# The row of 1/rms spread through DRAM instead of identity products, with a re-ordered start, in a two-layer encoder trunk

## The chip, the core and the metric

The kernel runs on one core of one Trainium2 chip. The metric is device time in microseconds for one launch; a figure for several runs is their median.

## What is computed

A trunk of two layers over 512 tokens of width 1024, all in float32. Each layer normalizes x, projects it to four branches and their gates, mixes them back and adds, then does the same with a convolutional feed-forward block:

```python
def _rmsnorm(x, g):
    y = xf * lax.rsqrt(jnp.mean(jnp.square(xf), axis=-1, keepdims=True) + EPS)
    return (y * g).astype(x.dtype)

for l in range(DEPTH):                      # DEPTH = 2, SEQ = 512, D_MODEL = 1024
    h = _rmsnorm(x, g_mix[l])
    proj = h @ w_in[l]                      # gates, conformer GLU, q/k/v of three attentions
    ...
    x = x + mixed @ w_out[l]
    x = x + _conv_ffn(_rmsnorm(x, g_ffn[l]), w_up[l], ffn_conv_w[l], ffn_conv_b[l], w_down[l])
```

## The kernel before

The activations stand transposed: eight tiles of 128 channels by 512 tokens. Each float32 operand is split into a rounded part and a remainder (xh and xl, w_hi and w_lo), and each product is made of three matmuls, hi by hi, hi by lo and lo by hi (L224 to L226, token-major L408 to L410).

**Weights** come in units of 128x1024 (`weights`, L189): a DMA into w_raw (two buffers), ScalarE rounds to w_hi (L204), VectorE subtracts to w_lo (L205), three buffers each. One unit feeds one block of 24 matmuls of 512 columns. `unit` (L209) keeps the next unit requested. The DMAs stand on SyncE's queue (SP), except the very first unit's, which comes in two halves on ScalarE's queue. Tiles of a pool with bufs=n go round in n buffers, and a writer waits for the readers of the buffer's last use. PSUM holds eight tiles of 128x512: four of mm, four of aux.

**Norms.** The factor 1/rms of a token is not applied to x; the products are made of x times the gain, and the factor is multiplied in behind them. `norm_tile` (L264) makes xh and xl of each tile and gathers the squares in sqacc. `finish_norm` (L281) sums sqacc over partitions with four matmuls by a column of ones (L293), so that token b*128+p stands on partition p, column b, and takes the inverse root on VectorE (`rsqrt`, L242): rstd, 128x4. Where tokens lie on partitions, rstd is used as it is. Where tokens lie along the row, in `glu`, `gates` and `ffn`, the factor is needed as RB, 128x512, the same row on each partition: before, VectorE scaled the identity by each column of rstd (L300), TensorE multiplied these four 128x128 tiles by the identity (L306), and ScalarE copied the result from PSUM to RB (L308). RB and sqacc share one buffer. `finish_norm` is called four times: at the start, between the mixing and the feed-forward in each layer, and at the start of layer 1. It is a generator, and `tick` (L731) advances all such side tasks: once in the middle of a block, once or more behind it. With delay 1 at a feed-forward the sums of squares come behind the first block.

**Feed-forward** (`ffn`, L776). Blocks come in pairs, gate and up. After each pair VectorE reads both PSUM tiles times RB into U (L796, shown below), ScalarE and VectorE do the three-tap convolution (L799 to L801), then swish and the product. Each block and the sums of squares take the next of the four mm tiles.

```python
                ps = pss[s]
                u = U[(2 * i + s) % 4]
                v.tensor_tensor(u[:, 1:513], ps, self.RB, ALU.mult)
```

**The start** (`run`, L817). ScalarE loads its table with a dummy exponential, POOL zeroes a tile z, and TensorE multiplies z by itself WARM times. x tile 0, sixteen columns of the parameters (the gains), x tile 1 and the others come on SP's queue. The order of instructions on each engine is set by a scheduler that follows the program's order and priorities; `issue_after` and the high priority of the weights shift it.

Of the kernel before, what the change touches and what calls it, by code (L numbers as in the profile page):

```python
# [14 lines left out]
F32 = mybir.dt.float32  # L15
F32R = mybir.dt.float32r
I32 = mybir.dt.int32
AF = mybir.ActivationFunctionType
ALU = mybir.AluOpType
# [3 lines left out]
P = 128  # L23
L = 2
D = 1024
S = 512
KT = D // P
NB = S // P
# [18 lines left out]
NCST = 1544  # L47


WARM = 9  # L50


PHASE = 24
# [127 lines left out]
class Trunk:  # L181
# [7 lines left out]
    def weights(self, upto, ahead=3000, parts=1, queue=None):  # L189

        nc = self.nc
        while self.w_emitted < min(upto, len(self.w_list)):
            l, off, n = self.w_list[self.w_emitted]
            with self.tc.high_priority(offset=ahead):
                raw = self.wpool.tile([P, 1024], F32, name="w_raw", tag="w_raw", bufs=2)
                hi = self.wpool.tile([P, 1024], F32R, name="w_hi", tag="w_hi", bufs=3)
                lo = self.wpool.tile([P, 1024], F32R, name="w_lo", tag="w_lo", bufs=3)
                src = self.W[l, off:off + n * P].rearrange("(p c) -> p c", p=P)
                for i in range(parts):
                    s = slice(i * n // parts, (i + 1) * n // parts)  # L200
                    (queue or nc.sync).dma_start(raw[:, s], src[:, s])
                for i in range(parts):
                    s = slice(i * n // parts, (i + 1) * n // parts)
                    nc.scalar.activation(hi[:, s], raw[:, s], AF.Copy)  # L204
                    nc.vector.tensor_tensor(lo[:, s], raw[:, s], hi[:, s].bitcast(F32), ALU.subtract)  # L205
            self.w_ready.append((hi, lo))
            self.w_emitted += 1
# [56 lines left out]
    def norm_tile(self, d, xn, pool):  # L264

        nc = self.nc
        g = self.par(self.norm_g, d)
        xh = self.xpool.tile([P, S], F32R, name=f"xh{d}", tag=f"xh{d}", bufs=1)
        xl = self.xpool.tile([P, S], F32R, name=f"xl{d}", tag=f"xl{d}", bufs=1)
        nc.scalar.activation(xh, xn, AF.Copy, scale=g)  # L270
        nc.vector.scalar_tensor_tensor(xl, xn, g, xh.bitcast(F32), ALU.mult, ALU.subtract)
        self.Xh.append(xh)
        self.Xl.append(xl)
        if d == 0:
            nc.scalar.activation(self.sqacc, xn, AF.Square)
        else:
            sq = pool.tile([P, S], F32, name="sq", tag="sq", bufs=2)
            nc.scalar.activation(sq, xn, AF.Square)
            nc.vector.tensor_tensor(self.sqacc, self.sqacc, sq, ALU.add)

    def finish_norm(self, delay):  # L281

        nc = self.nc
        sqacc = self.sqacc
        self.rstd = self.norm.tile([P, NB], F32, name="rstd", tag="rstd", bufs=2)
        rstd = self.rstd

        def work():
            for _ in range(delay):
                yield  # L290
            ps = self.mm()
            for b in range(NB):
                nc.tensor.matmul(ps[:, b:b + 1], lhsT=sqacc[:, b * P:(b + 1) * P],  # L293
                                 rhs=self.cst[:, C_ONE:C_ONE + 1], start=True, stop=True)
            v = self.norm.tile([P, NB], F32, name="ms", tag="ms", bufs=2)
            nc.vector.tensor_scalar(v, ps[:, 0:NB], 1.0 / D, EPS, ALU.mult, ALU.add)
            self.rsqrt(self.norm, v, [P, NB], rstd)
            dg = self.scratch()
            for b in range(NB):
                nc.vector.tensor_scalar(dg[:, b * P:(b + 1) * P], self.ident, 0.0, rstd[:, b:b + 1], ALU.mult, ALU.add)  # L300
            yield
            yield
            ps = self.aux()
            for b in range(NB):
                t = slice(b * P, (b + 1) * P)
                nc.tensor.matmul(ps[:, t], lhsT=dg[:, t], rhs=self.ident, start=True, stop=True)  # L306
            self.RB = self.norm.tile([P, S + PHASE], F32, name="RB", tag="RB", bufs=1)[:, :S]
            nc.scalar.activation(self.RB, ps, AF.Copy)  # L308
            yield

        self.side.append(work())
# [505 lines left out]
    def run(self):  # L817
        nc, tc = self.nc, self.tc
        with ExitStack() as st:
            pool = lambda name, **k: st.enter_context(tc.tile_pool(name=name, bufs=1, **k))  # L820
            self.const = pool("const")
            self.xpool = pool("xparts")
            self.wpool = pool("weights")
            self.norm = pool("norm")
            self.psum = pool("psum", space=PSUM)
            self.dram = pool("dram", space=bass.MemoryType.DRAM)
            self.w_list = []
            for l in range(L):
                off = 0
                for _, _, n in UNITS:  # L830
                    self.w_list.append((l, off, n))
                    off += n * P
            self.w_emitted = self.w_used = 0
            self.w_ready = []
            self.side, self.waiting, self.head = [], [], None

            self.cst = self.const.tile([P, NCST], F32, name="cst", tag="cst", bufs=1)
            self.ident = self.cst[:, C_ID:C_ID + P]
            self.prm = self.const.tile([P, NPAR], F32, name="prm", tag="prm", bufs=1)
            warm = self.const.tile([P, 1], F32, name="warm", tag="warm", bufs=1)  # L840
            nc.vector.memset(warm, 0.0)
            nc.scalar.activation(warm, warm, AF.Exp)
            with tc.tile_pool(name="first", bufs=1, reuse_waits="tile") as first:

                z = first.tile([P, S], F32R, name="zero", tag="zero", bufs=1)
                nc.gpsimd.memset(z.bitcast(F32), 0.0)
                ps = self.aux()
                for i in range(WARM):
                    nc.tensor.matmul(ps, lhsT=z[:, :P], rhs=z, start=True, stop=True)
                self.start_norm('g_mix')  # L850
                for d in range(KT):
                    xn = first.tile([P, S], F32, name="xn", tag="xn", bufs=8)
                    nc.sync.dma_start(xn, self.xT[d])
                    if d == 0:
                        nc.sync.dma_start(self.prm[:, 0:16], self.PAR[0][:, 0:16])
                        self.weights(1, 0, 2, nc.scalar)
                    self.norm_tile(d, xn, first)
                    if d in (1, 3):
                        self.weights(2 + d // 2, 0)
                    if d == 2:  # L860
                        nc.sync.dma_start(self.prm[:, 16:], self.PAR[0][:, 16:])
                nc.sync.dma_start(self.cst, self.CST)
                self.finish_norm(7)
            self.xres = [self.xT[d] for d in range(KT)]
            for l in range(L):
                self.layer(l)
# [5 lines left out]
    def layer(self, l):  # L872
# [2 lines left out]
        self.Y, self.mixed, self.MH, self.glu_u = [None] * 4, [], [], []  # L875
        with tc.tile_pool(name="gate", bufs=1, reuse_waits="tile") as self.gp:
            with tc.tile_pool(name="attn", bufs=1, reuse_waits="tile") as self.ap:
                self.scratch = lambda: self.gp.tile([P, S], F32, name="dg", tag="t1", bufs=2)
                late = lambda n: iter([None] * n)
                Q = self.project_qk(None, self.aux)  # L880
                self.derive_params()
                V = self.new_V()
                self.queue(chain(late(3 if l else 5), self.qk_norm(*Q, 4, 4, 0), self.attention(l, 'na', V, 1)))
                Vd = self.new_V()
                self.project_v(V, Vd)
                Q = self.project_qk(0)
                self.queue(chain(self.qk_norm(*Q, 4, 4, 2), self.attention(l, 'dil', Vd, 2)))
                self.glu()
                self.side.append(self.conv())
                V = self.new_V()  # L890
                Q = self.project_swa(V)
                self.queue(chain(self.qk_norm(*Q, 4, 2, 4), self.attention(l, 'swa', V, 3)))
                for n in ORDER[:3]:
                    self.gates(n)
                while self.side:
                    self.tick()
            with tc.tile_pool(name="outp", bufs=1, reuse_waits="tile") as self.op:
# [3 lines left out]
                for d in range(0, KT, 2):  # L901
# [3 lines left out]
                    for k0, k1 in zip(cuts, cuts[1:]):  # L905
                        for e in range(2):
                            if k0 == 0:
                                ws.append(self.unit())
                            hi, lo = ws[e]
# [6 lines left out]
                self.xres = self.xnew  # L916
                self.finish_norm(1)
        with tc.tile_pool(name="ffn", bufs=1, reuse_waits="tile") as self.fp:
            self.scratch = lambda: self.fp.tile([P, S], F32, name="dg", tag="cy0", bufs=2)
            F = self.ffn()  # L920
            if not last:
                self.load_prm(l + 1)
# [57 lines left out]
```

## Time and profile before

| | us |
|---|---|
| median of three runs | 1604.56 |
| lowest, highest | 1604.18, 1605.97 |
| the profiled execution, its own time | 1605.87 |
| span in its profile | 1604.1 |
| TensorE busy, matmuls | 1594.7 (99%) |
| VectorE, ScalarE, POOL busy | 1110.1, 778.6, 99.9 |

Times in the profile are microseconds from the first instruction; a matmul's time runs until its pipeline is empty, so starts, not durations, tell the pace of TensorE. DVE is VectorE, ACT ScalarE, SP SyncE, POOL GpSimd, PE TensorE; a name with q is the engine's sequencer, which also issues DMAs. L12 is line 12 of the kernel before; behind the change lines are numbered anew.

### The profile page before, as it was taken

The numbers are of one execution on the slowest core, as the hardware profiler recorded it, in microseconds if no ns is written. First come the engines' busy times: TensorE is split into PE (matmuls) and PEld (weight loads), VectorE is DVE, ScalarE is ACT, GpSimd is POOL, SyncE is SP. The second block draws the span as 40 slices with busy tenths as digits, with TensorE's granted clock in tenths as the row PEclk, the third lists the DMA queues.
The fourth block names the chain that finished last, engine by engine and source line by source line (L and its number), as shares of the span: only waits on it lengthen the run. The fifth ranks groups of instructions, "written<-read, shape, count | busy, mean of one in ns | idle before, by whom it ended". The sixth has DMA issues, their size and how long they took to land.

```text
span 1604.1 us, 19934 instructions
## 1 busy us (share of the span) xinstructions
PE 1594.7 (99%) x7425; PEld 1328.0 (83%) x7425; DVE 1110.1 (69%) x1860; ACT 778.6 (49%) x1303; POOL 99.9 (6%) x169
## 2 busy tenths in 40 slices
PE   9999999999999999999999999999999999999999
PEld 7888888888888888888888888888888888888887
DVE  6689888765677777843356889887556777777221
ACT  5677766433444444432237777662434444444211
POOL 0012001222000000000000110012210000000000
PEclk9999999999999999999999999999999999999999
DMA  6523232333533233233336322223326333333342
GB/s 206 182 92 90 71 88 78 93 97 97 181 112 104 93 94 104 89 128 129 126 111 182 105 67 87 83 66 105 105 93 187 106 102 92 102 95 91 122 135 74
DMA packets 57041, 174.95 MB, mean 109 GB/s; under 512 B 6768, under 2 KB 7024, under 8 KB 56944
## 3 DMA queue, kind: packets, MB, share of 16 engines
q1 hardware_dynamic: 56656, 173.16, 34.7%
q8 instruction: 58, 0.95, 0.2%
q10 hardware_dynamic: 288, 0.52, 0.1%
q14 instruction: 39, 0.32, 0.1%
HBM read 157.93 MB, written 10.49 MB: 105 GB/s over the span
## 4 chain that ended last, share of the span: by engine, by line
PE 92%; DVE 4%; ACT 2%; issue 1%; DMA 0%; SPq 0%; ACTq 0%; DVEq 0%
PE mm L224 25%; PE mm L226 25%; PE mm L225 25%; PE mm L408 2%; PE mm L410 2%; PE mm L409 2%; PE aux L629 1%; DVE w_lo L205 1%; PE aux L408 1%; PE aux L409 1%; PE aux L410 1%; PE aux L653 1%; PE aux L592 1%; PE aux L652 1%; PE aux L593 1%
## 5 line engine op out<-in xcount | busy, mean ns | idle before, releaser
L224 PE MATMUL mm<-xh,w_hi 128*128 128x512 f32 x1280 | 500.1, 391 | 0.0
L226 PE MATMUL mm<-xh,w_lo 128*128 128x512 f32 x1280 | 499.0, 390 | 0.0
L225 PE MATMUL mm<-xl,w_hi 128*128 128x512 f32 x1280 | 498.6, 390 | 0.0
L204 ACT ACTIVATE w_hi<-w_raw 128x1024 fp32r<-128x1024 f32 (+2 forms) x273 | 284.5, 1042 | 421.4 <-PE mm L225 344.3
L205 DVE TENSOR_TENSOR w_lo<-w_raw,w_hi 128x1024 fp32r<-128x1024 f32 (+2 forms) x273 | 330.1, 1210 | 160.3 <-ACT w_hi L204 156.4
L226 PEld LDWEIGHTS mm<-xh,w_lo 128*128 128x128 f32 x1280 | 240.3, 188 | 50.7
L224 PEld LDWEIGHTS mm<-xh,w_hi 128*128 128x128 f32 x1280 | 240.3, 188 | 49.2 <-ACT V L530 0.3
L225 PEld LDWEIGHTS mm<-xl,w_hi 128*128 128x128 f32 x1280 | 240.4, 188 | 48.6
L224 PE MATMUL mm<-fh,w_hi 128*128 128x512 f32 x352 | 136.9, 389 | 0.0
L225 PE MATMUL mm<-fl,w_hi 128*128 128x512 f32 x352 | 136.9, 389 | 0.0
L226 PE MATMUL mm<-fh,w_lo 128*128 128x512 f32 x352 | 136.9, 389 | 0.0
L346 DVE SCALAR_TENSOR_TENSOR cv<-cv,prm 128x512 f32<-128x512 f32 x120 | 93.6, 780 | 0.6
L723 POOL TENSOR_TENSOR mx<-mx,t 128x512 f32<-128x512 f32 x44 | 66.9, 1529 | 422.7 <-DVE t L722 413.8
L811 ACT ACTIVATE fh<-cy 128x512 fp32r<-128x512 f32 x44 | 27.8, 632 | 117.6 <-DVE cy L808 117.6
L765 DVE TENSOR_TENSOR xn<-mm,xr 128x512 f32<-128x512 f32 x32 | 22.1, 691 | 84.3 <-PE mm L226 81.2
L226 PEld LDWEIGHTS mm<-fh,w_lo 128*128 128x128 f32 x352 | 66.1, 188 | 13.8
L224 PEld LDWEIGHTS mm<-fh,w_hi 128*128 128x128 f32 x352 | 66.1, 188 | 13.7
L225 PEld LDWEIGHTS mm<-fl,w_hi 128*128 128x128 f32 x352 | 66.1, 188 | 13.7
L408 PE MATMUL mm<-w_hi,xh 128*128 128x512 f32 x192 | 76.4, 398 | 0.3 <-DVE V L531 0.2
L693 DVE TENSOR_TENSOR t<-mm,RB 128x512 f32<-128x512 f32 x64 | 44.0, 687 | 46.2 <-PE mm L226 45.8
L410 PE MATMUL mm<-w_hi,xl 128*128 128x512 f32 x192 | 75.1, 391 | 0.0
L409 PE MATMUL mm<-w_lo,xh 128*128 128x512 f32 x192 | 74.9, 390 | 0.0
(145 smaller groups left out, 2296.8 us busy)
## 6 DMA issues: line engine op xcount, KB each, us to landing
w_raw<-W SPq DMA_DIRECT2D x239, 512.0 KB, 3.6
w_raw<-W SPq DMA_DIRECT2D x32, 448.0 KB, 3.4
res<-xn SPq DMA_DIRECT2D x24, 256.0 KB, 2.0
xr<-res SPq DMA_DIRECT2D x24, 256.0 KB, 2.9
tab<-TB SPq DMA_DIRECT2D x8, 448.0 KB, 3.8
KH<-KH SPq DMA_DIRECT2D x20, 128.0 KB, 3.9
KL<-KL SPq DMA_DIRECT2D x20, 128.0 KB, 3.9
xn<-xT SPq DMA_DIRECT2D x8, 256.0 KB, 5.4
```

The lines of the kernel that those rows point to most:

```text
L204: nc.scalar.activation(hi[:, s], raw[:, s], AF.Copy)
L205: nc.vector.tensor_tensor(lo[:, s], raw[:, s], hi[:, s].bitcast(F32), ALU.subtract)
L224: mm(ps, lhsT=wh, rhs=xh, start=start, stop=False)
L225: mm(ps, lhsT=wh, rhs=xl, start=False, stop=False)
L226: self.last_mm = mm(ps, lhsT=wl, rhs=xh, start=False, stop=stop)
L346: self.after_mm(v.scalar_tensor_tensor(acc, u[:, t:t + S], w(t), acc, ALU.mult, ALU.add))
L408: mm(pss[b], lhsT=self.Xh[k][:, t], rhs=hi[:, s], start=k == 0, stop=False)
L409: mm(pss[b], lhsT=self.Xh[k][:, t], rhs=lo[:, s], start=False, stop=False)
L410: self.last_mm = mm(pss[b], lhsT=self.Xl[k][:, t], rhs=hi[:, s], start=False, stop=k == KT - 1)
L693: v.tensor_tensor(t1, ps, self.RB, ALU.mult)
L723: (v if n == ORDER[3] and d >= 6 else nc.gpsimd).tensor_tensor(m, m, t, ALU.add)
L811: nc.scalar.activation(fh, f, AF.Copy, scale=0.5)
```

## The change

The identity products, their scratch tile and ScalarE's copy are gone. POOL issues two DMAs instead: rstd into a row of 512 values in DRAM, and that row back to all 128 partitions of RB. At the start the sixteen parameter columns are issued on ScalarE's queue, ahead of the first weight's halves, instead of on SP's; the dummy exponential is placed behind those halves in the program; z is zeroed by VectorE; there are ten warm products instead of nine; and the square of x tile 0 is issued behind the first w_hi.

```diff
-WARM = 9
+WARM = 10
...
-                    nc.scalar.activation(hi[:, s], raw[:, s], AF.Copy)
+                    w = nc.scalar.activation(hi[:, s], raw[:, s], AF.Copy)
+                    self.first_hi = self.first_hi or w
...
         if d == 0:
-            nc.scalar.activation(self.sqacc, xn, AF.Square)
+            with self.tc.issue_after(self.first_hi.ins):
+                nc.scalar.activation(self.sqacc, xn, AF.Square)
...
-            dg = self.scratch()
-            for b in range(NB):
-                nc.vector.tensor_scalar(dg[:, b * P:(b + 1) * P], self.ident, 0.0, rstd[:, b:b + 1], ALU.mult, ALU.add)
-            yield
-            yield
-            ps = self.aux()
-            for b in range(NB):
-                t = slice(b * P, (b + 1) * P)
-                nc.tensor.matmul(ps[:, t], lhsT=dg[:, t], rhs=self.ident, start=True, stop=True)
+            row = self.dram.tile([S], F32, name="row", tag="row", bufs=2)
+            nc.gpsimd.dma_start(row.rearrange("(b p) -> p b", p=P), rstd)
             self.RB = self.norm.tile([P, S + PHASE], F32, name="RB", tag="RB", bufs=1)[:, :S]
-            nc.scalar.activation(self.RB, ps, AF.Copy)
+            nc.gpsimd.dma_start(self.RB, row.unsqueeze(0).broadcast_to([P, S]))
...
+            nc.scalar.dma_start(self.prm[:, 0:16], self.PAR[0][:, 0:16])
             warm = self.const.tile([P, 1], F32, name="warm", tag="warm", bufs=1)
             nc.vector.memset(warm, 0.0)
-            nc.scalar.activation(warm, warm, AF.Exp)
...
-                nc.gpsimd.memset(z.bitcast(F32), 0.0)
+                nc.vector.memset(z.bitcast(F32), 0.0)
...
                     if d == 0:
-                        nc.sync.dma_start(self.prm[:, 0:16], self.PAR[0][:, 0:16])
                         self.weights(1, 0, 2, nc.scalar)
+                        nc.scalar.activation(warm, warm, AF.Exp)
```

On ScalarE at the start, before (w_raw halves are the first weight unit, xh_105 and xh_112 are x tiles 0 and 1):

```order
L201 DMA w_raw<-W 128x512
L842 ACT_TABLE_LOAD
L842 ACTIVATE warm<-warm 128x1
L201 DMA w_raw<-W 128x512
L270 ACTIVATE xh_105<-xn,prm 128x512
L275 ACTIVATE sqacc<-xn 128x512
L204 ACTIVATE w_hi<-w_raw 128x512
```

and after the change:

```order
L836 DMA prm<-PAR 128x16
L201 DMA w_raw<-W 128x512
L852 ACT_TABLE_LOAD
L852 ACTIVATE warm<-warm 128x1
L201 DMA w_raw<-W 128x512
L271 ACTIVATE xh_106<-xn,prm 128x512
L204 ACTIVATE w_hi<-w_raw 128x512
L277 ACTIVATE sqacc<-xn 128x512
```

The parameters come in front of the weight's first half, and the square moves behind w_hi.

On VectorE at the feed-forward of layer 0, before (rstd is the last step of the inverse root, U_4529 and U_4532 are the first pair's tiles):

```order
L252 SCALAR_TENSOR_TENSOR rstd<-rs_q,rstd 128x4
L300 TENSOR_SCALAR dg<-cst,rstd 128x128 x4
L205 TENSOR_TENSOR w_lo<-w_raw,w_hi 128x1024
L796 TENSOR_TENSOR U_4529<-mm,RB 128x512
L796 TENSOR_TENSOR U_4532<-mm,RB 128x512
```

and after the change:

```order
L253 SCALAR_TENSOR_TENSOR rstd<-rs_q,rstd 128x4
L206 TENSOR_TENSOR w_lo<-w_raw,w_hi 128x1024
L791 TENSOR_TENSOR U_4522<-mm,RB 128x512
L791 TENSOR_TENSOR U_4525<-mm,RB 128x512
L795 SCALAR_TENSOR_TENSOR cy_4621<-U_4522,prm,cy_4621 128x512
L795 SCALAR_TENSOR_TENSOR cy_4629<-U_4525,prm,cy_4629 128x512
L796 SCALAR_TENSOR_TENSOR cy_4621<-U_4522,prm,cy_4621 128x512
L206 TENSOR_TENSOR w_lo<-w_raw,w_hi 128x1024
```

Only the scalings are gone in front of the first read of RB; one w_lo stands ahead of it, the next one five instructions behind.

On POOL at the same place, after the change (the memsets are the borders of the U tiles):

```order
L778 MEMSET U_4531 128x1
L301 DMA row<-rstd 128x4x1
L303 DMA RB<-row 128x512
L313 MEMSET cv 128x15
```

Before, the memset of U was followed directly by that of cv, which belongs to layer 1.

## Rows read from the trace of the kernel before

**Rows 1.** The page, part 1: busy us (share of the span) xinstructions, TensorE's matmuls.

```profile
PE 1594.7 (99%) x7425; PEld 1328.0 (83%) x7425; DVE 1110.1 (69%) x1860; ACT 778.6 (49%) x1303; POOL 99.9 (6%) x169
```

**Rows 2.** Waits of PE: engine line waited for: us in total, times, longest us.

```profile
PE aux L408 <- ACT w_hi L204: 1.2, 1, 1.2
```

**Rows 3.** Timeline of PE, first feed-forward: start us, us, engine line op out<-in.

```profile
455.26 0.39 PE L226 MATMUL mm<-xh,w_lo 128*128 128x512 f32 x1
455.49 1.05 PE L306 MATMUL aux<-cst,dg 128*128 128x128 f32 x8
456.30 0.48 PE L224 MATMUL mm<-xh,w_hi 128*128 128x512 f32 x1
...
461.84 0.39 PE L224 MATMUL mm<-xh,w_hi 128*128 128x512 f32 x1
```

**Rows 4.** Timeline of PE, start of layer 1.

```profile
823.87 0.39 PE L408 MATMUL aux<-w_hi,xh 128*128 128x512 f32 x1
...
825.05 0.48 PE L409 MATMUL aux<-w_lo,xh 128*128 128x512 f32 x1
```

**Rows 5.** Chain of waits, 0 to 14 us: start us, us, what.

```profile
1.18 3.60 DMA prm<-PAR
...
5.58 0.52 ACT sqacc L275
6.10 0.53 ACT w_hi L204
```

**Rows 6.** Timeline of ScalarE, first DMA issue.

```profile
0.73 0.41 ACTq L201 DMA_DIRECT2D w_raw<-W  x1
```

**Rows 7.** Timeline of PE, first 12 us; in brackets idle before, releaser.

```profile
1.30 4.21 PE L849 MATMUL aux<-zero 128*128 128x512 f32 x9 [1.30 <-POOL zero L846]
6.67 2.08 PE L408 MATMUL aux<-w_hi,xh 128*128 128x512 f32 x4 [1.16 <-ACT w_hi L204]
...
9.83 0.63 PE L410 MATMUL aux<-w_hi,xl 128*128 128x512 f32 x1
10.26 0.53 PE L409 MATMUL aux<-w_lo,xh 128*128 128x512 f32 x1
10.62 0.39 PE L410 MATMUL aux<-w_hi,xl 128*128 128x512 f32 x1
...
11.54 0.40 PE L409 MATMUL aux<-w_lo,xh 128*128 128x512 f32 x1
```

**Rows 8.** Stretches: length, busy of five engines, granted clock, DMA share, GB/s.

```profile
6.67:10.30 3.63, 3.62 (x9) 2.86 (x10) 3.63 (x8) 3.63 (x7) 0.00 (x0) 1.00 1.03 359
450.00:460.00 10.00, 10.00 (x49) 8.39 (x49) 6.93 (x21) 3.31 (x5) 0.00 (x0) 1.00 0.31 93
```

**Rows 9.** Timeline of VectorE, first feed-forward.

```profile
453.29 0.16 DVE L252 SCALAR_TENSOR_TENSOR rstd<-rs_q,rstd 128x4 f32<-128x4 f32 x1
...
456.60 1.23 DVE L205 TENSOR_TENSOR w_lo<-w_raw,w_hi 128x1024 fp32r<-128x1024 f32 x1 [2.24 <-ACT w_hi L204]
457.75 1.28 DVE L796 TENSOR_TENSOR U<-mm,RB 128x512 f32<-128x512 f32 x2
```

**Rows 10.** DMA issues: out<-in, queue, count, KB each, median us to landing.

```profile
res<-xn SPq DMA_DIRECT2D x24, 256.0 KB, 2.0
xr<-res SPq DMA_DIRECT2D x24, 256.0 KB, 2.9
...
V<-turn SPq DMA_DIRECT2D x2, 1024.0 KB, 5.8
...
w_raw<-W ACTq DMA_DIRECT2D x2, 256.0 KB, 3.9
...
prm<-PAR SPq DMA_DIRECT2D x1, 8.0 KB, 3.6
```

**Rows 11.** Timeline of VectorE, first 12 us.

```profile
7.94 0.68 DVE L205 TENSOR_TENSOR w_lo<-w_raw,w_hi 128x512 fp32r<-128x512 f32 x1
```

**Rows 12.** Timeline of POOL, before the first feed-forward.

```profile
405.30 0.10 POOL L783 MEMSET U<- 128x1 f32 x1
```

More of the change, by code (lines that the diff above doesn't have):

```diff
@@ L833, in run @@
             self.w_emitted = self.w_used = 0
+            self.first_hi = None
             self.w_ready = []
@@ L877, in layer @@
             with tc.tile_pool(name="attn", bufs=1, reuse_waits="tile") as self.ap:
-                self.scratch = lambda: self.gp.tile([P, S], F32, name="dg", tag="t1", bufs=2)
                 late = lambda n: iter([None] * n)
@@ L918, in layer @@
         with tc.tile_pool(name="ffn", bufs=1, reuse_waits="tile") as self.fp:
-            self.scratch = lambda: self.fp.tile([P, S], F32, name="dg", tag="cy0", bufs=2)
             F = self.ffn()
```

## The prediction

> **What bounds the kernel now.** I read the busy shares first, then what TensorE waited for, then the timeline at the places that the change touches. TensorE (PE) is busy for 1594.7 of 1604.1 us [rows 1], so an edit is worth something only if it shortens PE's own stream or makes PE wait. The list of PE's waits is short, and its longest single entries are at the start: 1.2 us for the first rounded weight [rows 2], and 1.30 before that for the zeroed tile [rows 7]; both lie in code that the change rewrites. The third kind of place is the identity products (L306). In the timeline at the first feed-forward block they are issued at 455.49, and the next product starts at 456.30 and takes 0.48 where its neighbours take 0.39 [rows 3]: they stand in PE's stream, not beside it. So there are three things to price: those products, the start, and the one place where the new route can make PE wait.
>
> **The identity products go.** Without them the product at 456.30 would start at 455.49: 0.81 us, and 0.09 for the long one behind it, 0.90 in all [rows 3]. In layer 1's start they split a triple: 823.87 to 825.05 is 1.18 where neighbours are 0.23 apart, so 0.95 and again 0.09, 1.04 [rows 3, 4]. The four places give 3 x 0.90 + 1.04 = **3.7 us**. The four VectorE scalings (L300) and ScalarE's copy (L308) go too; PE waits for neither, so I give them nothing.
>
> **The start.** The chain at the start reads: the small parameter DMA from 1.18 for 3.60 us, xh, the square, w_hi, then PE [rows 5]. The change puts that DMA first on ScalarE's queue, at 0.73 where the weight's first half is issued now [rows 6], so it would land 0.45 us earlier at the same 3.60; and the square moves behind w_hi, which takes its 0.52 out. The weight's half moves back one slot, from 0.73 to about 1.18, and with its 3.9 us [rows 10] it lands at about 5.1. That is just when xh would be done (6.67 - 0.45 - 0.52 = 5.70 for PE; less w_hi's 0.53 and 0.04 of hand-over is 5.13), so it holds w_hi by 0.05 to 0.1. PE's first real product comes at about 5.8 instead of 6.67: **0.9 us**, with 0.4 as the lower end if the extra DMA ahead of it merely delays the half (the DMA share just behind is already 1.03 [rows 8]), and 1.0 as the upper.
>
> The memset of z moves from POOL to VectorE behind a 128x1 memset, so PE's warm products may start some 0.1 later than 1.30. They are ten at 0.43 instead of nine, so they end near 5.7, where the real work begins. This matters only to the clock. The products from 6.67 on are 0.43 apart until 10.26, then 0.36 and from there 0.23, four steps from 10.62 to 11.54 [rows 7]: the ratio of 1.2 to 2.4 GHz, although the granted clock's column prints 1.00 [rows 8]. Eight steps of 0.43 and one of 0.36 cost 8 x 0.2 + 0.13 = 1.7 us over the fast pace. Before them PE worked from 1.30 to 5.51 and then stood idle for 1.16 us. With the gap closed the rise may come before the real work (1.7 gained) or as late after its start as now (nothing). No row shows an unbroken start, so I take the middle, **0.9 us**. The Trainium skill (TensorE: Matmul & The Clock Gate, section "Part 1: The HAM clock gate") says that activity releases the throttle and idleness brings it back; by that rule the closed gap would give back most of the 1.7, and the sum below would be 0.8 lower. The trace agrees as far as it goes: the rise came only in unbroken work behind the gap.
>
> Can PE be fed that much earlier? It would run up to 2.6 us ahead. The tightest input that I find is the second half's w_lo, which ends at 8.62 and is read by the product at 11.54 [rows 7, 11]: 2.9 us of slack. It holds, barely. SP's queue is also re-ordered (one slot less in front, one x tile ahead of two weights); those shifts are 0.45 us per slot and stay inside the same slack.
>
> **The detour through DRAM.** Two DMAs in a row on POOL replace products and copy: rstd to DRAM, and behind its landing the broadcast back into RB. At the first norm and at layer 1's start nobody hurries: RB is first read by the GLU, at least one whole projection of 96 products (96 x 0.23 = 22 us) later, and POOL's next work, the rope, needs that later projection too. The memsets ahead on POOL are no hindrance at the feed-forward: they ran at 405 [rows 12].
>
> At the two feed-forward starts the reader is near. rstd is done at 453.29 + 0.16 = 453.45; VectorE then does w_lo and at 457.75 the first L796, which reads RB and empties the PSUM tile of block 1 [rows 9]. The four mm tiles go round: block 1, the sums of squares, block 2, block 3; so **block 4 takes block 1's tile** and cannot start before that L796 ends. Block 4 starts at 461.84 now [rows 3], 460.94 without the 0.90. L796 takes 0.69 and its hand-over 0.05, so RB must land by 460.2: **6.7 us after rstd**. Layer 1 has the same schedule. Every microsecond beyond is a microsecond of PE, twice.
>
> No row shows a DMA issued by POOL or 4-byte runs. From below: a 256 KB store lands 2.0 us after issue and a 256 KB load after 2.9 [rows 10], 4.9 together: no wait. From above: the 8 KB of parameters, 64 bytes a row, took 3.6, and the read-back of a DRAM tile (1 MB) 5.8 [rows 10]: 9.4, a wait of 2.7 at each place. The row is small but in scraps, the broadcast has the bytes of the 256 KB load; I take the middle, 7.15, so 0.4 twice: **0.8 us lost**. The Trainium skill (DMA: Bandwidth & Descriptors, section "Anatomy of one DMA — SWDGE (gpsimd) path") fits a DMA from POOL as 2.0 us plus the bytes at 436 GB/s; as an estimate by that page, 2.0 and 2.6, nothing would be lost and the sum would be 0.8 lower.
>
> VectorE works in order, so while L796 waits for RB everything behind it stands: the other L796, the convolutions, the next w_lo. The w_lo in front (456.60) is for block 5, and the one behind is for block 6, whose need comes two blocks, some 11 us, after block 4's start; a delay of 3 us is covered. ScalarE's convolution step waits likewise, and its next w_hi behind it has the same room.
>
> **Sum.** 3.7 + 0.9 + 0.9 - 0.8 = 4.7 us. The profiled execution took 1605.87, of which 1604.1 are span, so it would come to 1601.2. The median of the runs shown is 1604.56, 1.31 lower. The runs spread over 1.8 us, about the size of the clock term; if they differ in just that, the median has part of the gain already. Half of the 1.31 is my choice: **1600.5**.
>
> **Rivals.**
> 1. *RB is early.* If the pair takes under 6.7, the lower bound's 4.9 and the clock give 1604.56 - 3.7 - 0.9 - 1.7 = 1598.3 at best; without the clock's part 1600.0. For it: small bytes, an idle POOL, a DMA share of 0.31 there [rows 8] would not slow it. Against: two landings in series and a queue not yet seen.
> 2. *RB is late by 1 to 2.7.* Then 2.0 to 5.3 are lost and 1604.56 - 5.5 + (2.0 to 5.3) is 1601.1 to 1604.4: the products removed are paid back in waits for PSUM. For it: the 64-byte rows' 3.6 for a mere 8 KB; against: those 3.6 fell into the rush of the start.
> 3. *Slower.* The row goes out as 512 scraps of 4 bytes. If scraps cost by number: 128 rows of 64 bytes took 3.6 where 128 rows of 2 KB took 2.0, so up to 1.6 per 128 and 6.4 for 512; 2.0 + 6.4 + 2.9 = 11.3 us, a wait of 4.6 at each block 4, 9.2 in all: 1604.56 - 5.5 + 9.2 = 1608.3. It outweighs the gains once the pair takes more than 6.7 + 2.75 = 9.5. The Trainium skill (DMA: Bandwidth & Descriptors, section "Rules for kernel authors") says that a strided last dimension becomes one descriptor per element; nothing in this trace shows such a DMA, and if the page holds, this is how it would hurt.
> 4. *The start gains nothing.* The DMA rush of the start sets w_hi's time, whatever the order. 1604.56 - 3.7 + 0.8 = 1601.7. Against: the square's 0.52 stood in the chain by itself.
>
> **Numbers.** Forecast (wait below 1 us per place) 0.45, rival 1 0.22, rival 2 0.17, rival 3 0.10, rival 4 0.06. A measurement of this kernel can tell about 0.2%, 3.2 us, from no change: faster is below 1601.3, slower above 1607.8. Of the forecast's case four fifths lie below 1601.3, with all of rival 1: 0.36 + 0.22 = 0.58, say 0.59. Its last fifth, rivals 2 and 4 lie within: 0.32. Rival 3 splits at 1607.8: 0.09 slower. The range runs from rival 1's best, 1598.3, to the upper end of rival 2, 1604.4; what is left out is rival 3 and scraps of the others.
>
> **What would show it.** L306 gone and the next block following at 0.23; the first real product near 5.8; the spacing 0.23 from early on; RB landing about 7 us after rstd; PE idle up to 1 us at block 4 of both feed-forwards, with L796 as its releaser. A wait there of more than 2.7 us, or a first product after 6.3, would make the prediction wrong.

## The result, and the profile after

The changed kernel takes **1610.29 us** (median of seven runs, 1609.5 to 1611.4) where the kernel before takes 1604.56 (seven runs, 1604.18 to 1606.23). The ratio is 1.0033, 95% interval 1.0021 to 1.0044: slower, by more than the 0.2% that a measurement can tell. The forecast was 1600.5 with a range that ended at 1604.4. It missed by 9.8 us and named the wrong sign. The runs of before lie in two groups 1.7 us apart; one of the experiments says why.

The page of the kernel after: part 1, then two groups of part 5, then three rows of part 6 (queue, count, KB each, median us from issue to landing).

```profile
PE 1593.2 (99%) x7394; PEld 1325.8 (82%) x7394; DVE 1103.0 (69%) x1845; ACT 774.8 (48%) x1299; POOL 104.5 (6%) x176
...
L225 PE MATMUL mm<-xh,w_hi 128*128 128x512 f32 x1280 | 501.6, 392 | 6.8 <-DVE U L791 6.8
...
L791 DVE TENSOR_TENSOR U<-mm,RB 128x512 f32<-128x512 f32 x88 | 60.4, 688 | 34.2 <-DMA RB<-row 22.5
...
RB<-row POOLq DMA_DIRECT2D x4, 256.0 KB, 5.2
...
row<-rstd POOLq DMA_DIRECT2D x4, 2.0 KB, 9.9
```

PE is busy for 1.5 us less than before [rows 1] in a span that is 4.4 us longer (1608.5 against 1604.1). So it stands idle where it did not. The second line says where: 6.8 us ahead of products of the block kind, released by L791. The third says what L791 waited for, and the last two price it: 2 KB take 9.9 us to land.

The waits of PE in the kernel after, the two that before did not have (us in total, times, longest):

```profile
PE mm L225 <- DVE U L791: 6.8, 2, 4.3
...
PE mm L403 <- DVE V L526: 0.7, 1, 0.7
```

The chain of waits at the first feed-forward, from 1/rms to PE (start us, us, what):

```profile
450.34 0.17 DVE rstd L253
...
450.80 9.45 DMA row<-rstd
...
460.82 4.40 DMA RB<-row
465.25 0.71 DVE U L791
...
466.09 0.47 PE mm L225
```

From the end of 1/rms at 450.51 to RB's landing at 465.22 is **14.7 us**. In layer 1 the same stretch takes 16.5. The forecast had 7.15.

PE's own timeline there (start us, us, engine line op; idle before in brackets):

```profile
446.15 0.95 PE L295 MATMUL mm<-cst,sqacc 128*128 128x1 f32 x8
...
457.98 0.39 PE L225 MATMUL mm<-xh,w_hi 128*128 128x512 f32 x1
...
463.19 0.39 PE L227 MATMUL mm<-xh,w_lo 128*128 128x512 f32 x1
466.09 0.47 PE L225 MATMUL mm<-xh,w_hi 128*128 128x512 f32 x1 [2.51 <-DVE U L791]
466.40 0.41 PE L226 MATMUL mm<-xl,w_hi 128*128 128x512 f32 x1
466.63 0.60 PE L227 MATMUL mm<-xh,w_lo 128*128 128x512 f32 x1
467.03 0.63 PE L225 MATMUL mm<-xh,w_hi 128*128 128x512 f32 x1
...
469.16 0.63 PE L227 MATMUL mm<-xh,w_lo 128*128 128x512 f32 x1
469.59 0.62 PE L225 MATMUL mm<-xh,w_hi 128*128 128x512 f32 x1
...
470.28 0.39 PE L227 MATMUL mm<-xh,w_lo 128*128 128x512 f32 x1
470.51 0.40 PE L225 MATMUL mm<-xh,w_hi 128*128 128x512 f32 x1
```

Two things are to be seen. Block 4, the third behind the sums of squares, begins at 457.98 with no wait, 7 us before any L791 has read block 1's tile. Blocks 1 to 3 hold three of the four mm tiles, so block 4 has the fourth, that of the sums of squares, emptied at 447: at this place the tiles of mm do not simply go round. The wait comes one block later. And behind the wait the products stand 0.43 apart (469.16 to 469.59) where they are 0.23 apart from 470.28 on: the clock had fallen. Here it fell just behind the idle stretch, not in it: the second and third product still came 0.23 apart (466.40 to 466.63). The stretches of the windows (length, PE busy, granted clock, DMA share, GB/s):

```profile
466.00:470.00 4.00, 3.91 (x10) 0.58 0.01 4
466.05:466.60 0.55, 0.51 (x2) 1.00 0.00 0
...
1265.70:1268.50 2.80, 2.79 (x7) 0.50 0.00 0
```

A granted clock of 0.50 is the lower of the two levels, 1.2 for 2.4 GHz. At 466 eight steps of about 0.43 cost some 1.6 us on top of the idle 2.51; in layer 1, where the products were slow from the first behind the wait, it is 4.26 us idle and some 1.4 of slow clock.

The start, for [rows 7], went in this execution as the forecast said:

```profile
1.49 4.58 PE L845 MATMUL aux<-zero 128*128 128x512 f32 x10 [1.49 <-DVE zero L842]
5.90 1.09 PE L403 MATMUL aux<-w_hi,xh 128*128 128x512 f32 x4
6.83 0.39 PE L404 MATMUL aux<-w_lo,xh 128*128 128x512 f32 x1
```

The first real product comes at 5.90 with no gap ahead, and the spacing is 0.23 from the first. In the eleven profiles of kernels with this start the first product comes between 5.83 and 6.49.

**Where the time went, stage by stage.** VectorE's first operation on each norm's sums of squares (L296 before, L298 after) is a mark that all kernels here share. Its four starts are read from VectorE's timeline and the end from the span. Differences of these make five stages:

| kernel | to norm 1 | to ffn 0 | to layer 1 | to ffn 1 | to the end | span |
|---|---|---|---|---|---|---|
| before | 31.35 | 418.73 | 360.90 | 434.56 | 358.56 | 1604.1 |
| after | 28.71 | 418.42 | 364.40 | 433.47 | 363.50 | 1608.5 |
| start_only | 29.66 | 418.86 | 360.89 | 434.57 | 358.42 | 1602.4 |
| detour_only | 29.47 | 417.40 | 363.72 | 433.49 | 360.52 | 1604.6 |
| runs16 | 30.43 | 419.86 | 359.99 | 435.37 | 357.55 | 1603.2 |
| perm_ffn | 29.14 | 419.68 | 359.97 | 435.36 | 357.55 | 1601.7 |
| perm_copy | 29.28 | 419.21 | 359.98 | 434.25 | 357.48 | 1600.2 |
| copy_all | 28.77 | 418.39 | 359.99 | 433.61 | 357.54 | 1598.3 |
| scraps_unused | 30.04 | 418.83 | 360.90 | 434.54 | 358.39 | 1602.7 |
| starts_scrap | 29.29 | 418.13 | 360.90 | 433.60 | 358.48 | 1600.4 |
| warm11 | 29.67 | 418.85 | 360.90 | 434.57 | 358.51 | 1602.5 |

After against before: 2.6 gained at the start, 0.3 and 1.1 at the two layer starts, and 3.5 and 4.9 lost in the two stages that begin with a feed-forward. The rows below the first two are the experiments. One profiled execution stands behind each row, and the first column moves by up to 1.7 us among kernels with the same start. The 2.6 holds against this execution of before, in which the first products came 0.43 apart [rows 7]; detour_only and warm11, which have the old order of the start, reach norm 1 at 29.47 and 29.67, start_only with the new one at 29.66.

### The profile page after: what moved, and what is told of

Read it like the earlier page. It is cut to its first block, busy times and chain, and to the rows that moved or that the text cites. A ratio compares the mean times of both kernels' runs of the same rounds, so it can differ in the third digit from the quotient of the medians.

```text
span 1608.5 us, 19872 instructions
## 1 busy us (share of the span) xinstructions
PE 1593.2 (99%) x7394; PEld 1325.8 (82%) x7394; DVE 1103.0 (69%) x1845; ACT 774.8 (48%) x1299; POOL 104.5 (6%) x176
## 3 DMA queue, kind: packets, MB, share of 16 engines
q0 software_dynamic: 448, 1.06, 0.3%
## 4 chain that ended last, share of the span: by engine, by line
PE 87%; DVE 5%; ACT 4%; DMA 3%; issue 1%; ACTq 0%; POOLq 0%; DVEq 0%
PE mm L225 25%; PE mm L227 24%; PE mm L226 24%; PE mm L403 2%; PE mm L405 2%; PE mm L404 2%; DVE w_lo L206 1%; PE aux L624 1%; DMA row<-rstd 1%; PE aux L403 1%; PE aux L405 1%; PE aux L404 1%; PE aux L648 1%; ACT w_hi L204 1%; PE aux L587 1%
## 5 line engine op out<-in xcount | busy, mean ns | idle before, releaser
L794 ACT ACTIVATE cy<-U,prm 128x512 f32<-128x512 f32 x88 | 71.2, 811 | 49.4 <-DVE U L791 48.6
L791 DVE TENSOR_TENSOR U<-mm,RB 128x512 f32<-128x512 f32 x88 | 60.4, 688 | 34.2 <-DMA RB<-row 22.5
L688 DVE TENSOR_TENSOR t<-mm,RB 128x512 f32<-128x512 f32 x64 | 44.0, 687 | 46.2 <-PE mm L227 45.8
```

The source lines that it names most:

```text
L794: nc.scalar.activation(y, u[:, 1:513], AF.Identity, scale=w(1), bias=self.par('ffn_conv_b', c))
```

## The experiments

Theory 1 at the outset: the row's 512 runs of 4 bytes are what costs; they make the pair of DMAs outlast block 5's deadline. That deadline, read after the result, is 12.2 us behind 1/rms: block 5 could start at 463.4, 12.9 after 450.5, less L791's 0.69 and its hand-over. The rivals are the start, POOL's queue as such, and the traffic of the scraps.

**start_only: the new start, the old identity products.** The diff of the change without its part in `finish_norm` and `scratch`.

> The start of the changed kernel with the identity products of the kernel before. Theory 1 (the row's 512 runs of 4 bytes are what cost): the start keeps its gain of 0.8 us and the clock its 1.7 us against the profiled 1605.87, so about 1603.4 (1602.5 to 1604.4), first product at 5.9, no stall over 0.5 us at either ffn. Rival (the new start does harm later): 1607 or more.

Measured: 1603.93 (11 runs, 1603.13 to 1604.76), ratio 0.9989 (0.9980 to 0.9998). The time is as theory 1 had it; the start harms nothing. The first product is not. It was put at 5.9 and came at 6.49, behind a gap:

```profile
6.49 1.20 PE L410 MATMUL aux<-w_hi,xh 128*128 128x512 f32 x4 [0.37 <-ACT w_hi L204]
```

The first half of the first weight took 4.62 us to land in this execution, where the prediction had 3.9.

**detour_only: the old start, the new detour.**

```
-            dg = self.scratch()
...
+            row = self.dram.tile([S], F32, name="row", tag="row", bufs=2)
+            nc.gpsimd.dma_start(row.rearrange("(b p) -> p b", p=P), rstd)
+            nc.gpsimd.dma_start(self.RB, row.unsqueeze(0).broadcast_to([P, S]))
```

> The start of the kernel before with the detour through DRAM. Theory 1: the two waits for U at the ffns come as in the changed kernel (2.5 and 4.3 us, with slow clock after each), so the changed kernel's 1610.3 plus the start's 0.8 and up to 1.7 of clock: 1611.1 to 1612.8. Rival (the loss belongs to the start): 1601 to 1603, which is before less the identity products' 3.7.

Measured: 1609.0 (10 runs, 1606.36 to 1610.22), ratio 1.0020 (1.0011 to 1.0029). The loss belongs to the detour; the size was put some 2 to 4 us too high. The profiled execution, at 1606.36 the fastest, has 4.3 us of waits where the changed kernel has 6.8; what the slower ones have is not shown:

```profile
PE mm L224 <- DVE U L789: 4.3, 2, 2.5
```

Its second wait also shows that a wait does not always bring the slow clock. In the first feed-forward the clock fell behind 1.81 us of idleness, in layer 1 it stayed at 1.00 behind 2.46 (stretch, length, PE busy, granted clock, DMA share, GB/s):

```profile
1260.55:1262.95 2.40, 0.00 (x0) 1.00 0.05 17
1263.00:1268.00 5.00, 5.00 (x22) 1.00 0.00 0
```

**runs16: fewer, longer runs.** The row in the order in which the partitions hold it; RB is then read in steps of 16 bytes in L318, L325, L688 and L791.

```
-            nc.gpsimd.dma_start(row.rearrange("(b p) -> p b", p=P), rstd)
+            nc.gpsimd.dma_start(row.rearrange("(p b) -> p b", p=P), rstd)
...
+            self.RB = self.RB.rearrange("q (p b) -> q b p", b=NB)
```

> The changed kernel, with the row in the order in which the partitions hold it: 128 runs of 16 bytes in place of 512 of 4, and the three kinds of multiplications read RB in steps of 16 bytes. Theory 1 (time goes with the count of runs): 2.0 us and a quarter of the other 7.9, so the row lands in 4 us, the pair takes 8 to 9 of the 12.2 us that block 5 leaves, no wait for U over 0.5 us: 1610.3 less the 10.2 us that both waits cost, 1600.1 (1599.3 to 1601.5). Rival (POOL's queue is slow whatever it writes): row 9 to 10 us, 1610. Rival (multiplications with steps of 16 bytes are slower, over 800 ns for 688): the 88 of them lie beside PE, so under 1 us more.

Measured: 1603.82 (11 runs, 1602.99 to 1604.97), ratio 0.9990 (0.9981 to 0.9998). POOL's timeline at the first feed-forward, and the two groups of multiplications:

```profile
453.95 0.59 POOL L305 DMA_DIRECT2D row<-rstd  x1 [52.97 <-DVE rstd L257]
456.82 0.55 POOL L307 DMA_DIRECT2D RB<-row  x1 [2.28 <-DMA row<-rstd]
```

```profile
L693 DVE TENSOR_TENSOR t<-mm,RB 128x512 f32<-128x512 f32 x64 | 69.0, 1079 | 39.6 <-PE mm L231 39.2
L796 DVE TENSOR_TENSOR U<-mm,RB 128x512 f32<-128x512 f32 x88 | 93.0, 1058 | 5.6 <-DMA RB<-row 5.6
```

POOL waits 2.28 us for the row where it waited 9.23, so its queue is not slow as such, and there is no wait for U. But the gain is 3.7 us short. The multiplications take 1058 to 1079 ns for 687. In the feed-forward stages that costs nothing (359.99 and 357.55 in the table); in the two stages with the attention, 419.86 and 435.37 are 1.5 and 1.8 more than copy_all's. There PE's waits for VectorE's results in L592 come to 5.6 us, where start_only's, in L594, are 2.8:

```profile
PE aux L592 <- DVE yf L659: 3.0, 4, 1.0
PE aux L592 <- DVE ptl L636: 1.7, 2, 1.4
...
PE aux L592 <- DVE mx L606: 0.9, 3, 0.5
```

"Beside PE" was true of 88 of them and not of the rest. The Trainium skill (SBUF — State Buffer, section "Door 1: The DMA port swizzle (why `[64,N]` ≈ `[32,N]`)") says that SBUF is read in lines of 16 bytes and that each access to a new line pays; these operations, four bytes out of every 16, agree: 1.54 to 1.57 times as long.

**probe_rows and probe_gap: what in the row costs?** A row that nobody uses beside the identity products, and a read-back of one number, so that POOL's next issue waits for the landing. The four norms get four shapes of row.

```
+            nc.gpsimd.dma_start(dst, src)
+            nc.gpsimd.dma_start(chk[:, 0:1], row[0:1].unsqueeze(0))
```

> The kernel start_only with a row that nobody uses, written at each of the four norms on POOL's queue and one number of it read back (so that the next issue waits for its landing): 256 runs of 8 bytes at the first, 512 of 4 at the first ffn, 128 of 16 at layer 1's start, 512 of 4 with 32 bytes from one to the next at the last. Theory 1: about 6, 10, 4 and 10 us. Rival (POOL's queue): 9 to 10 for all four. Rival (bytes side by side in one place of DRAM collide): the last far under 10. Time: theory 1 within 1 us of start_only; if the scraps starve the weights of PE, waits for w_hi over 0.5 us beside them.

The read-backs in POOL's timeline of probe_rows: 256 runs of 8 bytes, 512 of 4, 128 of 16, 512 of 4 with 32 bytes from start to start.

```profile
37.97 0.53 POOL L308 DMA_DIRECT2D chk<-row  x1 [3.40 <-DMA row<-rstd]
464.23 0.52 POOL L308 DMA_DIRECT2D chk<-row  x1 [8.40 <-DMA row<-rstd]
823.02 0.52 POOL L308 DMA_DIRECT2D chk<-row  x1 [2.98 <-DMA row<-rstd]
1259.81 0.52 POOL L308 DMA_DIRECT2D chk<-row  x1 [2.24 <-DMA row<-rstd]
```

The last line fells theory 1 in its form. The same 512 runs, spread out, are waited for as briefly as 128. Time 1616.85 (one run), 12.9 over start_only without a new wait of PE; shift32 below takes that up.

> As probe_rows, always 512 runs of 4 bytes, from the start of one to the next 16 bytes at the first norm, 32 at the first ffn, 8 at layer 1's start and 4 at the last; the tile of the read-back is 64 bytes wide instead of 32. Theory (it is not the count of the runs but neighbours in one stretch of DRAM that wait for each other): from issue to the next issue less POOL's own 0.8, about 2.5, 2.2, 4 and 9 us. Rival (the count decides, and the one sight of 2.2 us was chance): 8 to 10 us for all. Time: 1604 if a shift of the later tiles by 64 bytes is harmless where one by 32 bytes cost 12 us, else 1610 to 1617.

The read-backs of probe_gap, always 512 runs of 4 bytes, 16, 32, 8 and 4 bytes from start to start:

```profile
36.30 0.55 POOL L306 DMA_DIRECT2D chk<-row  x1 [2.10 <-DMA row<-rstd]
456.63 0.53 POOL L306 DMA_DIRECT2D chk<-row  x1 [2.36 <-DMA row<-rstd]
820.03 0.53 POOL L306 DMA_DIRECT2D chk<-row  x1 [3.64 <-DMA row<-rstd]
1261.31 0.54 POOL L306 DMA_DIRECT2D chk<-row  x1 [8.59 <-DMA row<-rstd]
```

So it is not the count. What costs is that 4-byte runs from different partitions lie side by side: 8.6 us at 4 bytes, 3.6 at 8, about 2.2 from 16 on. The 256 runs of probe_rows, whose starts are 8 bytes apart too, were waited for 3.40, as long as 512 at that distance. That neighbours in one stretch of DRAM wait for each other is the reading that fits; how the memory does it no run here shows. Time 1609.69 (one run): 64 bytes more in the norms' pool cost less than 32, but not nothing.

**scraps_unused: the traffic without a reader.** start_only with the dense row written at all four norms and read by nobody.

> The kernel start_only with the row of 512 runs of 4 bytes written at each of the four norms and read by nobody. Theory (the scraps harm through the wait for RB; beside it they slow the weights' transfers, 3.6 to 9.4 us, which two tiles of look-ahead nearly cover): 1603.9 to 1605.2, waits for w_hi or V of 1 us in all or less. Rival (the harm is the traffic itself): 1608 to 1612.

Measured: 1604.09 (11 runs, 1603.25 to 1605.92), ratio 0.9989 (0.9981 to 0.9998), the same as start_only's. The traffic by itself costs nothing that can be measured, although it may delay a transfer beside it: in the changed kernel's chain a weight at the first norm took 8.76 us to land, where the median is 3.6, ahead of the 0.7 us that PE waited for V.

**starts_scrap: the change's detour where nobody hurries.** The dense row at the two layer starts; identity products at the feed-forwards.

> The kernel start_only, with the detour as the change writes it (512 runs of 4 bytes, RB read straight) at the two layer starts alone; the two ffns keep their identity products. Theory (the scraps cost only where a reader of RB stands in PE's way within 12 us): the row takes 9 to 10 us, nobody waits for RB, the two places give what the products' removal is worth in PE's stream: 1603.9 less 1.9, 1602.0 (1601.2 to 1603.2, the upper end if the scraps delay a weight at the first norm by 1 us as in the changed kernel). Rival (scraps cost wherever they are written): 1604 or more.

Measured: 1602.6 (10 runs, 1601.16 to 1604.15), ratio 0.9979 (0.9970 to 0.9989). POOL's timeline at the first norm:

```profile
32.96 0.92 POOL L314 DMA_DIRECT2D row<-rstd  x1 [10.69 <-DVE rstd L253]
43.04 0.56 POOL L316 DMA_DIRECT2D RB<-row  x1 [9.16 <-DMA row<-rstd]
```

The same 9 us, and a gain of 0.7 and 1.0 at the two places (418.13 and 433.60 against start_only's 418.86 and 434.57). So the slow row harms here only where its reader stands in PE's way.

**perm_ffn and perm_copy: 16-byte runs and RB read straight.** At the feed-forwards the sums of squares are taken over every fourth column, so that the row is in the order of the tokens by itself; perm_copy also has the detour at the layer starts, with a copy on POOL.

```
-                                 lhsT=sqacc[:, b * P:(b + 1) * P]
+                                 lhsT=sqacc[:, b::NB] if ffn else sqacc[:, b * P:(b + 1) * P]
...
+                nc.gpsimd.dma_start(raw, row.unsqueeze(0).broadcast_to([P, S]))
+                nc.gpsimd.tensor_copy(self.RB.rearrange("q (b p) -> q b p", b=NB), raw.rearrange("q (p b) -> q b p", b=NB))
```

> The kernel start_only; at the two ffns alone the detour, with the sums of squares taken over every fourth column (partition p holds tokens 4p to 4p+3), so that the row's 128 runs of 16 bytes are in the order of the tokens and RB is read straight. The layer starts keep the identity products. Theory (it was the steps of 16 bytes, 1058 for 688 ns in 88 multiplications and 1079 for 687 in 64, that ate in runs16 what the products' removal gave): multiplications at 688 ns, no wait for U over 0.5 us, 1603.9 less two times 0.9: 1602.1 (1601.2 to 1603.0). Rival (a detour loses the 0.9 in another way, traffic or the products' own cover): 1603.9.

> As perm_ffn, and at the two layer starts the detour with 128 runs of 16 bytes into a scratch tile, put in the order of the tokens by one copy on POOL. No identity products are left. Theory: 1603.9 less 3.7, 1600.2 (1599.3 to 1601.5). Rival (as for perm_ffn): 1603 to 1604.

Measured: perm_ffn 1603.55 (1602.97 to 1604.56), ratio 0.9986 (0.9977 to 0.9995), which is the rival's 1603.9 rather than my 1602.1; perm_copy 1602.32 (1601.46 to 1602.92), ratio 0.9977 (0.9968 to 0.9986), which is neither's. PE's timeline, start_only first, then perm_ffn:

```profile
447.53 0.95 PE L295 MATMUL mm<-cst,sqacc 128*128 128x1 f32 x8
```

```profile
446.98 1.80 PE L295 MATMUL mm<-cst,sqacc 128*128 128x1 f32 x8
```

The eight weight loads in steps of 16 bytes take 0.85 us longer, in PE's stream, and give back what the identity products' removal gains. The Trainium skill (SBUF — State Buffer, the section named above) states its lines of 16 bytes without naming weight loads; these eight agree with it.

**copy_all: the copy everywhere, the sums of squares as before.** The changed kernel with its start; the lines taken out are those of the kernel before.

```
-            for b in range(NB):
-                nc.vector.tensor_scalar(dg[:, b * P:(b + 1) * P], self.ident, 0.0, rstd[:, b:b + 1], ALU.mult, ALU.add)
...
+            nc.gpsimd.dma_start(row.rearrange("(p b) -> p b", p=P), rstd)
+            raw = self.scratch()
+            nc.gpsimd.dma_start(raw, row.unsqueeze(0).broadcast_to([P, S]))
...
+            nc.gpsimd.tensor_copy(self.RB.rearrange("q (b p) -> q b p", b=NB), raw.rearrange("q (p b) -> q b p", b=NB))
```

> The detour at all four norms with 128 runs of 16 bytes into a scratch tile and one copy on POOL (1.09 us) into the order of the tokens; the sums of squares again over blocks of columns that lie side by side. Theory (in perm_ffn and perm_copy the sums of squares' weight loads in steps of 16 bytes took 1.80 us where they took 0.95, at each ffn, and that gave back the 0.9 of the identity products): 1602.3 less 1.7, 1600.6 (1599.8 to 1601.4); the copy ends some 8 us after 1/rms, before the 12.2 us at which block 5 wants its tile, no wait for U over 0.5 us. Rival (perm_copy's gain has another bound, so that only the layer starts count): 1602.3.

Measured: **1600.82** (8 runs, 1600.05 to 1601.84), ratio 0.9973 (0.9963 to 0.9983). It beats both kernels. POOL's timeline at the first feed-forward (the scratch tile is named dg):

```profile
450.82 0.59 POOL L301 DMA_DIRECT2D row<-rstd  x1 [48.36 <-DVE rstd L253]
453.42 0.55 POOL L303 DMA_DIRECT2D dg<-row  x1 [2.01 <-DMA row<-rstd]
457.61 1.08 POOL L307 COPY RB<-dg 128x512 f32<-128x512 f32 x1 [3.64 <-DMA dg<-row]
```

The copy ends at 458.69, some 8 us after 1/rms and 4 ahead of the deadline. The detour with this layout is 9.5 us faster than with the change's (1610.29).

**warm11: the two groups of before.** WARM = 11 for 9 in the kernel before, nothing else.

> The kernel before with 11 products on zeros at the start for 9, nothing else: they end at 6.45 where those ended at 5.51 and the first product began at 6.67. Theory (before's runs lie in two groups, 1604.0 to 1604.5 and 1605.7 to 1607, because the idle 1.16 us at the start lets the clock fall in some runs and not in others; the new start takes that away): all runs in one group, 1604.0 to 1604.7. Rival (the two groups have another cause): two groups as before, median 1605.9.

Measured: 1604.5 (11 runs, all from 1604.10 to 1604.97), ratio 0.9996 (0.9987 to 1.0005). One group, at the place of before's lower one, while 18 runs of before beside it split nine and nine (1604.11 to 1604.90, 1605.76 to 1606.37). So the start as it was lets the clock lag in some runs of before and not in others: detour_only's profile has the same start with a gap of 1.07 us, and its products stand 0.23 apart from 7.62 on, where those of before stand 0.43 apart. Whether it is the shorter gap or the longer work ahead of it that ends this, warm11 cannot tell; it changes both. The start is worth 1.7 us against the upper group; start_only's 1603.9 is 0.6 below warm11, in a separate comparison, and their profiles reach norm 1 at the same time, so what it gives beyond the clock is no firm number.

**shift32: what cost the probes their 12 us.** start_only with a tile of 32 bytes per partition in the pool of the norms, and no DMA.

```
+            chk = self.norm.tile([1, 8], F32, name="chk", tag="chk", bufs=1)
+            nc.gpsimd.memset(chk, 0.0)
```

> The kernel start_only with a tile of 32 bytes in the pool of the norms, set to zero by POOL at each norm, no transfer. Theory (in probe_rows it was the place of the later tiles in SBUF, shifted by 32 bytes, that took 12 us, in products that read fh and mh; not the transfers): 1615 to 1618, products of fh from 389 to 395 ns, no wait beside them. Rival (the read-back and the rows cost it): 1603.9.

Measured: 1615.95 (4 runs, 1615.65 to 1617.14), ratio 1.0067 (1.0051 to 1.0082). Groups of start_only, then of shift32:

```profile
L225 PE MATMUL mm<-fh,w_hi 128*128 128x512 f32 x352 | 136.9, 389 | 0.0
```

```profile
L225 PE MATMUL mm<-fh,w_hi 128*128 128x512 f32 x352 | 139.1, 395 | 0.0
```

No wait is longer but those for the first weights, by 0.9 us in all. The products that read fh and fl, 352 of each of three kinds, from a pool that is laid out after the norms', take 6 ns more each; those of mh and ml take 6 and those of yh and yl some 4 to 6, 128 of each kind. That makes some 11 of the 12 us. The products of xh, whose pool is laid out ahead of the norms', stay at 390 to 391. So here the place of a tile in SBUF set PE's pace; the transfers of the probes did not.

## Why the prediction was wrong

- **The identity products**, 3.7 forecast. Right. The stages without them are shorter by 0.90 and 0.88 at the feed-forwards (359.99 and 357.54 against start_only's 360.89 and 358.42) and by 0.96 in layer 1's start. At the first norm it is 0.5 to 0.7. That makes 3.3 us.
- **The start and its clock**, 0.9 and 0.9. In the changed kernel's trace the first product came at 5.90 for a forecast of 5.8. That was in part luck: the forecast has the first half of the weight land after 3.9 us, and where it took 4.62 (start_only) the product came at 6.49, behind the 6.3 that the prediction had set as a sign of being wrong. The slack of 2.9 us for the second half was used up in some traces too (in runs16 PE waited 0.17 and 0.22 for it). The clock term was half of its real size: "I take the middle" stood for an all-or-nothing term, and warm11 shows that all of the 1.7 comes back. Against the median, which lay in before's lower group, it was worth nothing, as the prediction feared.
- **The detour**, 0.8 lost. Wrong by about 9.6, and this decides. copy_all has the same stages without a wait: 364.40 - 359.99 and 363.50 - 357.54 make 4.4 and 6.0, **10.4 us**. Two steps failed, in opposite directions.
  - *"From above: ... 9.4"*. The pair took 14.7 and 16.5 us, far over the bound. The bound took its scraps from rows of 64 bytes [rows 10], and the nearest row was not near: 2 KB in 4-byte neighbours take 9.9 us to land, and even the broadcast, "the bytes of the 256 KB load", took 5.2 for 2.9 (4.0 in copy_all).
  - *"The four mm tiles go round"*. Here they did not. Block 4 took the tile of the sums of squares, free since 447, so the budget was 12.2 us and not 6.7. By the true budget even my upper bound of 9.4 would have cost nothing.
  - And the price of a late RB was more than its lateness. With both waits of this trace came the lower clock, some 1.6 and 1.4 us, which no term of mine or of a rival had.
- **Rival 3** had the late RB and the sign, with 11.3 us for the pair and 1608.3 for the whole. That the time came so near was luck, of two errors against each other: by the true budget of 12.2 us its own 11.3 would have cost nothing, and the pair took 14.7 and 16.5. Its reason, "if scraps cost by number", fell: spread by 32 bytes, the same number is waited for 2.2 to 2.4 us. The Trainium skill (DMA: Bandwidth & Descriptors, section "Rules for kernel authors") says that a strided last dimension becomes one descriptor per element. It gives no price for one; with a fixed price the spread rows would have cost as much as the dense ones, and in probe_gap they cost 2.1 us for 8.6. The Trainium skill's two-part fit that the prediction cited (the same page, section "Anatomy of one DMA — SWDGE (gpsimd) path"), by estimate 2.0 and 2.6 us, is near for rows of 16-byte runs, which are waited for 2.0 to 3.3 behind an issue of 0.6, off by a factor of five for the dense row, and too low for the broadcast (3.8 to 5.2). Rival 3 was given 0.10 because nothing in the trace showed scraps; that was a reason for a wide range, not for a small chance.
- **Rivals 1, 2 and 4** fell. RB was late, the two places cost 4.4 and 6.0 us where rival 2 had up to 2.7 each, and the start gained at least the clock (start_only's 1603.93 for 1606.09 of before beside it).

What stays open: why 4-byte neighbours are slow, why the 256 KB broadcast takes 3.8 to 5.2 us where the like load from SP takes 2.9, and what decides whether a wait brings the slow clock.

## What to carry to other kernels

A DMA that scatters single numbers is priced by how its runs lie in memory, not by its bytes: keep each partition's numbers together (16 bytes were enough here) and put them in order afterwards on an idle engine, not in the operands that the busy engines read over and over. For a detour's deadline find which tile the next block really takes, from who waits for whom in the trace, and allow for the clock that an idle TensorE can lose. Where no row is near the cost of a new operation, the range belongs to both signs.

## What was not expected

- 512 runs of 4 bytes from POOL: waited for 8.4 to 10.3 us at 4 bytes from start to start, 3.6 at 8, 2.1 at 16, 2.2 to 2.4 at 32.
- PE's granted clock fell to its lower level behind an idle stretch of 2.5 us, when two products had already come at the fast pace, and the next eight came about 0.43 apart; behind 2.46 us of idleness in detour_only it did not fall.
- Weight loads in steps of 16 bytes: 1.80 us for eight products that take 0.95; VectorE's multiplications with one such operand: 1.06 to 1.08 us for 0.69.
- A tile of 32 bytes that moves the later pools: 12 us, 0.75%, twice what the change itself did.
